# Running log-sum-exp over a sequence: the new last row is summed in place, one Ln takes all rows of a chunk, and GpSimd copies a part of that row to the work tile

## The chip, the cores and the metric

The kernel runs on one core of one Trainium2 chip. The metric is the device time in microseconds (us), the median of the runs shown. Engines are named as in the profile: PE is TensorE, DVE is VectorE, ACT is ScalarE, POOL is GpSimd, SP is SyncE, which here issues every transfer.

## The reference

The input x has 4 sequences of 4096 rows, each row with 4128 float32 numbers. The output is the running log-sum-exp along the rows.

```python
out[:, 0, :] = x[:, 0, :].copy()
for t in range(1, S):
    mx = np.maximum(out[:, t - 1, :], x[:, t, :])
    out[:, t, :] = mx + np.log(np.exp(out[:, t - 1, :] - mx) + np.exp(x[:, t, :] - mx))
```

## The kernel before

The kernel computes Ln of a running sum of Exp(x). At the end it tests from sums collected on the way (`probe`, `short`) whether the range of float32 was kept, and runs a slow general form if it was not.

The work is cut into 49 steps. A step takes r = 2 or 3 consecutive rows for each of the 128 partitions, all 4128 columns: partition p holds rows p·r to p·r + r − 1 of the block. A 2-row tile has 4128 KB (4.227 MB), a 3-row tile 6192 KB (6.340 MB). The lists `begin`, `usual` and `final` give r for each step: the first sequence begins 2, 2, 2, 3, 2, 3, and the last one ends 3, 3, 2, 2. Four tiles (`slots`) are used in turn; each is loaded, worked on in place and stored from.

Within a step there are three chunks of 1376 columns. In the texts chunks are numbered through: step 0 has chunks 0 to 2, step 1 has 3 to 5. A chunk goes through five operations:

- `exp` (line 102, ACT): Exp of all r rows in place. In the first step of a sequence line 105 adds a small check.
- `sums` (DVE): for three rows line 114 adds row 0 to row 1 in place. Then line 116 writes the sum of all the partition's rows to partitions 0 to 126 of the work tile `z`. Partition 127 of `z` keeps the last total of the step before.
- `head` (line 124, PE): a matrix product with a triangular matrix gives in PSUM, for each partition, the sum of all that comes before it, with the carried total from partition 127.
- `add` (DVE): line 133 adds that base from PSUM to rows 0 to r − 2. Line 141 adds rows r − 2 and r − 1 and writes the new last row to `z` (line 136, with the sum for `probe`, in the last step of a sequence).
- `log` (ACT): line 146 takes Ln of rows 0 to r − 2 in place, line 147 takes Ln of `z` and writes it to row r − 1.

The order on each engine is written out by hand in lists and fixed under a manual schedule. For most steps `usual_turn` gives this order. On ACT: Ln of chunk i, Exp of chunk i + 3, Ln of chunk i + 1, Exp of chunk i + 4, and so on. On DVE: add of chunk i, sums of chunk i + 2, add of chunk i + 1, sums of chunk i + 3. `last_turns` changes this for the last steps. SP's queue carries, in order, store t (line 91, after the three `log` of step t) and then load t + 3 (line 88, after store t − 1, which frees its tile). Steps 0 to 3 are loaded at the start; store 1 is issued ahead of load 4.

`needs` is a table from which the program order is derived; the waits themselves follow from what each instruction reads and writes. GpSimd sets constants and zeroes `z` at the start (lines 44 to 69) and has nothing after that.

Of the kernel before, what the change touches and what calls it, by code (L numbers as in the profile page):

```python
# [9 lines left out]
ACT = mybir.ActivationFunctionType  # L10
ALU = mybir.AluOpType
AX = mybir.AxisListType
P = 128
MM = 512
NC = 3
SLOTS = 4
SMALL = 2.0 ** -63
LARGE = 2.0 ** 62
# [3 lines left out]
def kernel(  # L22
# [5 lines left out]
    nc = tc.nc  # L28
    B, S, D = x.shape
    assert S % P == 0 and D % (NC * 32) == 0  # L30
    CH = D // NC
    cuts = [(s, min(s + MM, CH)) for s in range(0, CH, MM)]
# [13 lines left out]
        out=below, in_=below, pattern=[[1, P]], compare_op=ALU.is_ge,  # L46
# [5 lines left out]
        out=carried, in_=below, pattern=[[0, P]], compare_op=ALU.not_equal,  # L52
# [4 lines left out]

    probe = consts.tile([P, B * NC], FP32, name="probe")
    nc.gpsimd.memset(probe, 1.0)

    short = consts.tile([1, B * NC], FP32, name="short")
    spare = consts.tile([1, CH + 8], FP32, name="spare")[:, :CH]
# [3 lines left out]

    z = [zpool.tile([P, CH], FP32, name=f"z{c}") for c in range(NC)]
    for t in z:
        nc.gpsimd.memset(t, 0.0)  # L69

    slots = [x2.tile([P, 2, D], FP32, name="x0")]
    slots += [x3.tile([P, 3, D], FP32, name=f"x{k}") for k in range(1, SLOTS)]
    sides = [ppool.tile([P, CH], FP32, name=f"p{k}") for k in range(2)]
# [19 lines left out]
    class Chunk:  # L93
        def __init__(self, step, c):
            self.t, self.c, self.z = step, c, z[c]
            self.pt = sides[(step.n * NC + c) % 2]
            self.cols = slice(c * CH, (c + 1) * CH)
# [30 lines left out]
        def add(self):  # L128
            t, r = self.t, self.t.r
            k = t.b * NC + self.c  # L130
            e = t.xt[:, 0:r - 1, self.cols]
            base = self.pt.unsqueeze(1).to_broadcast([P, r - 1, CH])
            nc.vector.tensor_tensor(out=e, in0=base, in1=e, op=ALU.add)  # L133
            ends = (t.xt[:, r - 2, self.cols], t.xt[:, r - 1, self.cols])
            if t.last:
                nc.vector.tensor_tensor_reduce(  # L136
                    out=self.z, in0=ends[0], in1=ends[1], scale=1.0, scalar=0.0,
                    op0=ALU.add, op1=ALU.add, accum_out=probe[:, k:k + 1],
                )
            else:  # L140
                nc.vector.tensor_tensor(out=self.z, in0=ends[0], in1=ends[1], op=ALU.add)  # L141

        def log(self):
            t, r = self.t, self.t.r
            e = t.xt[:, 0:r - 1, self.cols]
            nc.scalar.activation(e, e, ACT.Ln)  # L146
            nc.scalar.activation(t.xt[:, r - 1, self.cols], self.z, ACT.Ln)  # L147

    begin = [2, 2, 2, 3, 2, 3, 2, 3, 2, 3, 3, 3, 2]
    usual = [3, 2, 3, 2, 3, 3, 3, 2, 3, 3, 3, 2]  # L150
# [2 lines left out]
    for b in range(B):  # L153
        row = 0
        for r in final if b == B - 1 else usual if b else begin:
            if row == S:
                break
            steps.append(Step(b, row, r, slots[len(steps) % SLOTS], row + P * r == S))
            steps[-1].n = len(steps) - 1
# [5 lines left out]

    moves = [("load", t) for t in range(SLOTS)]
    ahead = SLOTS
    for t in range(n):
# [25 lines left out]
    for t in range(n):  # L194
        exps, sums = last_turns.get(t, usual_turn)
# [11 lines left out]
    def needs(what, t, c=None):  # L207
        if what == "load":
            return [("store", t - SLOTS)]
        if what == "store":  # L210
            return [("log", t, c) for c in range(NC)]
        return {
            "exp": [("load", t)],
            "sums": [("exp", t, c), ("log", t - 1, c)],
            "head": [("sums", t, c), ("add", t - 1, c)],
            "add": [("head", t, c)],
            "log": [("add", t, c)],
        }[what]

    done, at = set(), {e: 0 for e in lists}  # L220
    while any(at[e] < len(l) for e, l in lists.items()):
        before = len(done), sum(at.values())
        for e, l in lists.items():
            while at[e] < len(l):
                op = l[at[e]]
                if op[1] < n:
                    if any(0 <= d[1] and d not in done for d in needs(*op)):
                        break
                    done.add(op)
                    of = steps[op[1]]  # L230
                    getattr(of if len(op) == 2 else of.chunks[op[2]], op[0])()
                at[e] += 1
        assert before != (len(done), sum(at.values()))
# [5 lines left out]
        out=fits[:, :B * NC], in0=probe, scalar1=LARGE, scalar2=None, op0=ALU.is_le,  # L239
    )  # L240
    nc.vector.tensor_scalar(
        out=fits[0:1, B * NC:], in0=short, scalar1=0.0, scalar2=None, op0=ALU.is_le,
# [7 lines left out]
        out=flag, in0=good, scalar1=float(P), scalar2=None, op0=ALU.is_lt,  # L250
# [62 lines left out]
```

## Time and profile before

| | |
|---|---|
| device time, median of 3 runs | 1260.83 us (1260.6 to 1261.09) |
| span of the profiled execution (first to last instruction) | 1258.4 us |
| what lies around the span, against the median | 2.4 us |
| ACT busy | 955.4 us |
| DVE busy | 956.2 us |
| PE busy | 602.4 us |
| POOL busy | 4.6 us |
| bytes moved by DMA, mean rate | 541.28 MB, 430 GB/s |
| ACT L146 and L147, Ln, mean of one | 2045 ns and 1334 ns |
| DVE L141, new last row, mean of one | 1592 ns |
| store 0, store 1, store 2, store 48 issued at | 38.04, 52.73, 70.28, 1239.89 us |

The profile is of one execution. Times in it are counted from the start of its span; the time of a whole execution is the span and what lies around it. Its groups mix shapes where a line has two: L146 takes 1376 elements a partition in a 2-row step and 2752 in a 3-row step. A transfer is shown where it is issued; its landing is later.

### The profile page before, as it was taken

To read this page: it belongs to the slowest core of one execution; us is meant where nothing else is said; L and a number is where in the kernel's file an instruction comes from. 1 tells how busy PE (TensorE), PEld (TensorE's weight loads), DVE (VectorE), ACT (ScalarE), POOL (GpSimd) and SP (SyncE) were. 2 spreads that over 40 slices of the span, in tenths; PEclk is the share of its full clock that TensorE was granted. 3 is DMA by queue.
4 is the path that set the end of the run, shared out by engine and by line. 5 is a ranking of instruction groups with operands and counts; after the bars stand their busy time and mean duration, and the time that the engine had idled before them with its cause. 6 is when DMAs were issued, how large, how long until landed. Compare 5 with 4: busy or idle time off the path is not lost.

```text
span 1258.4 us, 3228 instructions
## 1 busy us (share of the span) xinstructions
PE 602.4 (48%) x884; PEld 233.1 (19%) x884; DVE 956.2 (76%) x548; ACT 955.4 (76%) x466; POOL 4.6 (0%) x14
## 2 busy tenths in 40 slices
PE   3654454453535455345364535634535553463361
PEld 1221121121212122112121212211211211121120
DVE  3997696795967699579596679957957976795792
ACT  6987687786976699578697668866968966896792
POOL 1000000000000000000000000000000000000000
PEclk9877776676677667666676666766766776676676
DMA  9999999999999999999999999999999999999998
GB/s 403 420 439 426 432 436 428 432 437 429 439 425 438 430 437 433 436 435 427 440 422 436 436 432 434 434 430 435 437 428 437 431 435 431 434 437 433 432 435 354
DMA packets 14131, 541.28 MB, mean 430 GB/s; under 512 B 1568, under 2 KB 1568, under 8 KB 1568
## 3 DMA queue, kind: packets, MB, share of 16 engines
q1 hardware_dynamic: 14112, 541.07, 99.6%
q8 instruction: 7, 0.11, 0.0%
q14 instruction: 12, 0.10, 0.0%
HBM read 270.53 MB, written 270.53 MB: 430 GB/s over the span
## 4 chain that ended last, share of the span: by engine, by line
DMA 69%; ACT 14%; DVE 13%; PE 1%; issue 1%; SPq 0%; ACTq 0%; DVEq 0%
DMA x<-in_x_dram 52%; DMA out_dram<-x 17%; ACT x L102 6%; DVE x L133 5%; ACT x L146 5%; DVE z L116 3%; ACT x L147 3%; DVE z L141 3%; DVE x L114 2%; PE p L124 1%; SPq L91 0%; DVE z L136 0%; ACTq L146 0%; ACTq L254 0%; SPq L88 0%
## 5 line engine op out<-in xcount | busy, mean ns | idle before, releaser
L124 PE MATMUL p<-z,carried 128*128 128x512 f32 (+1 forms) x810 | 551.8, 842 | 544.3 <-DVE z L116 544.3
L102 ACT ACTIVATE x<-x 128x4128 f32<-128x4128 f32 (+1 forms) x147 | 468.0, 3187 | 219.7 <-DMA x<-in_x_dram 219.7
L124 PEld LDWEIGHTS p<-z,carried 128*128 128x128 f32 x810 | 213.4, 280 | 882.2 <-DVE z L116 648.3
L133 DVE TENSOR_TENSOR x<-p,x 128x2752 f32<-128x2752 f32 (+1 forms) x147 | 361.9, 2462 | 6.2 <-PE p L124 6.2
L146 ACT ACTIVATE x<-x 128x2752 f32<-128x2752 f32 (+1 forms) x147 | 300.6, 2045 | 63.5 <-DVE z L141 58.5
L114 DVE TENSOR_TENSOR x<-x 128x1376 f32<-128x1376 f32 x90 | 142.9, 1588 | 216.5 <-ACT x L102 216.5
L116 DVE TENSOR_TENSOR z<-x 127x1376 f32<-127x1376 f32 x147 | 233.9, 1591 | 53.8 <-ACT x L102 49.4
L141 DVE TENSOR_TENSOR z<-x 128x1376 f32<-128x1376 f32 x135 | 215.0, 1592 | 4.6
L147 ACT ACTIVATE x<-z 128x1376 f32<-128x1376 f32 x147 | 196.0, 1334 | 0.0
L124 PE MATMUL p<-z,below 128*128 128x512 f32 (+1 forms) x72 | 50.4, 864 | 87.4 <-DVE z L116 87.4
L124 PEld LDWEIGHTS p<-z,below 128*128 128x128 f32 x72 | 19.6, 289 | 117.7 <-DVE z L116 78.8
L136 DVE CUSTOM_DVE_ANT_0 z<-x 128x1376 f32<-128x1376 f32 x12 | 19.1, 1592 | 0.4
L105 ACT ACTIVATE spare<-x,tiny 1x1376 f32<-1x1376 f32 x12 | 17.3, 1442 | 0.5
L69 POOL MEMSET z<- 128x1376 f32 x3 | 3.7, 1241 | 0.0
L105 ACT ACTIVATION_READ_ACCUMULATOR spare<-x,tiny 1x1 f32 x12 | 2.2, 186 | 0.0
L247 PE MATMUL good<-ones,low 128*1 128x1 f32 x2 | 0.2, 164 | 3.8 <-DVE low L245 3.8
L34 ACT ACT_TABLE_LOAD x1 | 1.3, 1283 | 0.8 <-PEq L297 0.8
L136 DVE DVE_READ_ACCUMULATOR2_ANT probe<- 128x1 f32 x12 | 1.0, 83 | 0.0
L247 PEld LDWEIGHTS good<-ones,low 128*1 128x1 f32 x2 | 0.1, 80 | 4.8 <-DVE low L245 4.8
L249 DVE TENSOR_SCALAR flag<-good 1x1 int32<-1x1 f32 x1 | 0.1, 148 | 0.3 <-PE good L247 0.3
L51 POOL TENSOR_SCALAR_AFFINE_SELECT carried<-below 128x128 f32<-128x128 f32 x1 | 0.3, 290 | 0.0
L45 POOL TENSOR_SCALAR_AFFINE_SELECT below<-below 128x128 f32<-128x128 f32 x1 | 0.3, 285 | 0.0
(13 smaller groups left out, 1.6 us busy)
## 6 DMA issues: line engine op xcount, KB each, us to landing
x<-in_x_dram SPq DMA_DIRECT2D x30, 6192.0 KB, 38.4
out_dram<-x SPq DMA_DIRECT2D x30, 6192.0 KB, 25.0
x<-in_x_dram SPq DMA_DIRECT2D x19, 4128.0 KB, 33.0
out_dram<-x SPq DMA_DIRECT2D x19, 4128.0 KB, 21.6
```

What stands on the lines that cost most here:

```text
L34: nc.scalar.preload_act_table_set("natural_log_exp_and_others")
L69: nc.gpsimd.memset(t, 0.0)
L102: nc.scalar.activation(e, e, ACT.Exp)
L105: nc.scalar.activation(spare, t.xt[0:1, 0, self.cols], ACT.Relu, bias=tiny, scale=-1.0, accum_out=short[:, k:k + 1],)
L114: nc.vector.tensor_tensor(out=e[1], in0=e[0], in1=e[1], op=ALU.add)
L116: nc.vector.tensor_tensor(out=self.z[0:n], in0=e[r - 2][0:n], in1=e[r - 1][0:n], op=ALU.add,)
L124: nc.tensor.matmul(pt[:, a:b], lhsT=w, rhs=self.z[:, a:b], start=True, stop=True,)
L133: nc.vector.tensor_tensor(out=e, in0=base, in1=e, op=ALU.add)
L136: nc.vector.tensor_tensor_reduce(out=self.z, in0=ends[0], in1=ends[1], scale=1.0, scalar=0.0, op0=ALU.add, op1=ALU.add, accum_out=probe[:, ...
L141: nc.vector.tensor_tensor(out=self.z, in0=ends[0], in1=ends[1], op=ALU.add)
L146: nc.scalar.activation(e, e, ACT.Ln)
L147: nc.scalar.activation(t.xt[:, r - 1, self.cols], self.z, ACT.Ln)
```

## The change

The new last row is written in place, to row r − 1 of the tile, instead of to `z`. So one Ln takes all r rows of a chunk, and line 147 of before is gone. Since `head` of the next step still needs the last total in partition 127 of `z`, GpSimd copies partitions 96 to 127 of the new row to `z`, in every step but the last of a sequence (135 copies). `sums` of the next step then writes over partitions 0 to 126. Ln overwrites the row that the copy reads, so Ln waits for the copy; `sums` writes where the copy wrote, so it waits for the copy too. The order of the remaining instructions on PE, DVE, ACT and SP is the one of before. In the changed file the lines from 16 on stand one lower, those of `add` after the branch differ: line 142 is the new last row, line 143 the copy, line 147 the Ln.

```diff
+TOP = 96
...
             if t.last:
                 nc.vector.tensor_tensor_reduce(
-                    out=self.z, in0=ends[0], in1=ends[1], scale=1.0, scalar=0.0,
+                    out=ends[1], in0=ends[0], in1=ends[1], scale=1.0, scalar=0.0,
                     op0=ALU.add, op1=ALU.add, accum_out=probe[:, k:k + 1],
                 )
             else:
-                nc.vector.tensor_tensor(out=self.z, in0=ends[0], in1=ends[1], op=ALU.add)
+                nc.vector.tensor_tensor(out=ends[1], in0=ends[0], in1=ends[1], op=ALU.add)
+                nc.gpsimd.tensor_copy(out=self.z[TOP:], in_=ends[1][TOP:])

         def log(self):
-            t, r = self.t, self.t.r
-            e = t.xt[:, 0:r - 1, self.cols]
+            e = self.t.xt[:, :, self.cols]
             nc.scalar.activation(e, e, ACT.Ln)
-            nc.scalar.activation(t.xt[:, r - 1, self.cols], self.z, ACT.Ln)
...
-            "sums": [("exp", t, c), ("log", t - 1, c)],
+            "sums": [("exp", t, c), ("add", t - 1, c)],
```

## The prediction

> **What bounds the kernel now.** I read the page's engine shares first, then its slices and DMA rows, then the waits, then the stretches that lead up to the first and the last stores, and last the timeline of VectorE, ScalarE and SyncE.
>
> The head of the page and its DMA part:
>
> ```profile
> PE 602.4 (48%) x884; PEld 233.1 (19%) x884; DVE 956.2 (76%) x548; ACT 955.4 (76%) x466; POOL 4.6 (0%) x14
> ...
> DMA  9999999999999999999999999999999999999998
> ...
> q1 hardware_dynamic: 14112, 541.07, 99.6%
> ```
>
> VectorE and ScalarE are each idle for a quarter of the span; the one queue's transfers fill it. So 541.07 MB over the DMA engines is the bound (433 GB/s over 100 to 1170 us), and only a stretch in which the queue runs dry adds time. Work saved on ScalarE or VectorE cannot shorten it.
>
> The waits say the same from the other end (columns: who waited, for whom, us in total, times, longest):
>
> ```profile
> ACT x L102 <- DMA x<-in_x_dram: 219.7, 43, 11.9
> ...
> ACT x L146 <- DVE z L141: 58.5, 65, 5.0
> ```
>
> What must be known is how near the queue comes to running dry. At each store I take the bytes issued so far (a 2-row tile is 4.227 MB, a 3-row tile 6.340) less the bytes moved, from stretches that begin at 0 and end at the issue (columns: length, busy time of PE, PEld, DVE, ACT, POOL, clock, DMA share, GB/s):
>
> ```profile
> 0.00:52.73 52.73, 24.31 (x44) 10.07 (x45) 32.17 (x21) 40.29 (x28) 4.64 (x14) 0.94 0.98 410
> 0.00:70.28 70.28, 35.04 (x60) 13.97 (x60) 48.02 (x31) 57.38 (x37) 4.64 (x14) 0.88 0.98 414
> 0.00:92.87 92.87, 47.16 (x81) 18.93 (x82) 70.25 (x43) 76.83 (x46) 4.64 (x14) 0.86 0.99 421
> ...
> 0.00:1239.89 1239.89, 602.36 (x884) 233.11 (x884) 956.23 (x548) 955.36 (x466) 4.64 (x14) 0.69 1.00 432
> ```
>
> Store 1 at 52.73: issued 23.25 MB (four loads, store 0), moved 0.410 x 52.73 = 21.62, left 1.63 MB, at 430 GB/s 3.8 us. So the queue would run dry at 56.5. In the same way store 2 has 6.1 us in hand, store 3 7.4, and the last store, at 1239.89, about 2.8. In mid-run the stores come with 5 to 13 us in hand. The margins are thin in two places: the first three stores, whose steps run as fast as ScalarE and VectorE let them, and the end.
>
> The timeline of ScalarE in the first stretch (start, us, engine, line, shape):
>
> ```profile
> 30.48 1.33 ACT L146 ACTIVATE x<-x 128x1376 f32<-128x1376 f32 x1
> 31.72 1.33 ACT L147 ACTIVATE x<-z 128x1376 f32<-128x1376 f32 x1
> 32.96 2.48 ACT L102 ACTIVATE x<-x 128x2752 f32<-128x2752 f32 x1
> 35.42 1.35 ACT L146 ACTIVATE x<-x 128x1376 f32<-128x1376 f32 x1
> ```
>
> It shows no gap, and a chunk every 4.9 us. VectorE beside it:
>
> ```profile
> 33.74 1.59 DVE L141 TENSOR_TENSOR z<-x 128x1376 f32<-128x1376 f32 x1
> 35.48 1.59 DVE L116 TENSOR_TENSOR z<-x 127x1376 f32<-127x1376 f32 x1
> ```
>
> L141 ends at 35.33, and L146, which needs it, starts at 35.42. The next sums start at 35.48, as the Exp they need ends. Whatever is put between L141 and the Ln lies on the path.
>
> **The change, part by part.** *Last row in place (L141, L136).* Same operands in, another place out: 1592 ns stays, cost nothing, and nothing has to hide it.
>
> *One Ln in place of two.* 147 instructions fewer. The two start 2.50 us apart from the next Exp (30.48 to 32.96), where one instruction on 2752 elements has a pitch of 2.40 (48.7 us of ScalarE's idle time already falls ahead of L146, so little of the 147 x 0.10 = 15 us can show). It counts where ScalarE sets the pace: 0.1 us a chunk.
>
> *Sums wait for the copy, not for the Ln.* The page has no wait of L116 on L147, so that gains nothing. The copy of a chunk is issued a whole add ahead of the next sums on that z (4.8 us for two rows), so the new wait is covered unless the copy takes longer than that.
>
> *The GpSimd copy, 135 times.* GpSimd is otherwise empty after 5.3 us, so nothing queues behind a waiting copy but the next copy. The Ln now waits for it, since it overwrites the row that the copy reads; behind the Ln on ScalarE is queued the next step's Exp, behind that the sums, and behind the third chunk's Ln the store on SP's queue, with the next load after it. The trace has no copy. From below, a memset that only writes:
>
> ```profile
> L69 POOL MEMSET z<- 128x1376 f32 x3 | 3.7, 1241 | 0.0
> ...
> L51 POOL TENSOR_SCALAR_AFFINE_SELECT carried<-below 128x128 f32<-128x128 f32 x1 | 0.3, 290 | 0.0
> ```
>
> From above, the affine select, which reads and writes: less the 98 ns of the smallest memset it is 1.50 ns an element, so 0.10 + 1376 x 1.50 = 2.16 us. A copy does no comparing and is nearer to the memset: I take 1.4, and 0.1 for one more hand-off (L141 to L146 takes 0.09), 1.5 together. Both ends stay open, and no gain is possible, since the Ln waits for more than before. The Trainium skill ("GPSIMD Engine Reference", § 4.1 Engine selection) calls one-input operations there roughly line-rate; at its 1.2 GHz an estimate is 1.15 us, which would make each sum below some 0.5 us smaller; no run so far shows a copy.
>
> *What that does to the pace.* The orders close a ring over two chunks: Ln of chunk i, Exp of i+3, sums of i+3, both adds of i+2, Ln of i+2. Two rows, now: 2.50 + 2.56 + 1.50 + 1.62 + 1.68 = 9.9, and the trace has 35.42 - 25.60 = 9.8. With the copy: 9.8 - 0.1 + 1.5 = 11.2. Three rows: 15.2 becomes 16.6, while the queue takes 19.7 for two such chunks and 13.1 for two 2-row chunks. So the copy alone does not change the bound of mid-run.
>
> *Where the copy falls.* It is released at the end of L141. In this ring that is, for every other chunk, the moment at which the next sums start on VectorE, an add with two SBUF operands. The trace has no GpSimd read beside a VectorE add: its memsets are over at 5.3 us, the first add starts at 15.67. If the two take turns, the copy waits 1.6 us more (the add's 1.59; with three rows it gets in between L114 and L116), or holds the add up by its own 1.4. The ring is then 11.2 + 1.6 = 12.8 for two rows and 18.2 for three, still under 13.1 and 19.7. Sharing of any kind, a turn for either or both slowed, costs about this; only full independence costs none. I take the turns.
>
> **The sum, with turns.** First stretch: Ln of chunk 0 from 25.60 to 28.6 (sums until 27.06, copy), then every second 12.8 later: chunk 2 at 41.4, 4 at 54.2, 6 at 67.0. Chunks 1, 3, 5 follow 4.8 behind: 33.4, 46.2, 59.0. Store 1 comes at 59.0 + 2.5 = 61.5, 5.0 us after the queue runs dry at 56.5. Store 1 and load 4 are 8.45 MB or 19.7 us, to 81.2. The Exp behind the Ln of chunk 6 is the first with three rows and ends at 73.0; sums (3.2) and the adds of chunk 8 (3.2) end at 79.5, its copy waits out L114 and its Ln starts at 82.6, so store 2 goes out at 85.1: 3.9 dry. Store 2 and load 5 last 24.6 us, to 109.7; the Ln of chunk 11 starts at 107.1, store 3 at 110.8: 1.1 dry. Together 10.0.
>
> Mid-run: a store that follows a landing is delayed by 1.5 + 1.6 = 3.1 us, against at least 4.7 in hand. The store after it comes at the engines' pace, three chunks of 9.1 instead of 7.3 (271.69 to 293.50), so 5.5 + 3.1 = 8.6 late against 12 in hand. Nothing.
>
> End, from the last but two loads' landing at 1178.72: no copies in the last step, but the ring over the two steps ahead delays store 47 by 5.3 us against 4.9 in hand, and the last by 4.2 against 2.8: about 1.5.
>
> Sum: 11.5 on 1258.4, the span, is 1269.9. The profiled execution's span lies 2.4 below the median of 1260.83, which I keep: **1272**. Its own range is 1266 (the copy at 1.24 and short turns) to 1280 (2.16).
>
> **The rivals.** *No turns: not slower.* Copy and add run side by side. The ring is 11.2; Ln of chunk 5 starts at 54.5, store 1 at 57.0 (0.5 dry), store 2 at 77.6 against 76.7 (0.9), store 3 at 100.6 against 102.3, the end 1.1 late with 2.8 in hand. That is +1.4, 1262, within 0.2% (2.5 us, about what a measurement of this kernel can tell from no change). For it: VectorE's adds stay within 1583 to 1594 ns whatever ScalarE, PE and the queue do beside them. Against: none of these is GpSimd. It tips at a copy of 1.7 us; at 2.16 it is +4.5, 1265.
>
> *The turn covers both sums of a three-row step.* The 30 ns between L114 and L116 may be too short for GpSimd to get in. Then the three-row ring is 19.8, and 20.5 with the dear copy, against 19.7: mid-run is bound by the engines. Over 45 pairs of chunks that is 6 to 36 us more, and 3 in the first stretch: 1281 to 1311, about 1290.
>
> On turns as such, the Trainium skill ("SBUF — State Buffer", § Who interferes with whom) says that a Vector instruction with two SBUF inputs contends with a GpSimd instruction that reads SBUF, and that the second one blocks for the whole instruction. By that rule one of the two slower cases holds; no run here shows it yet.
>
> *Faster.* Needs the queue to move bytes faster, as nothing else bounds. The 10-us stretches swing between 404 and 466 GB/s with no pattern that later stores would change: to 1257, and little chance.
>
> **How the numbers follow.** Turns between single instructions 0.52; turns over both sums 0.10; independent with a cheap copy 0.26, with a dear one 0.08; faster 0.04. Slower by over 0.2% is 0.52 + 0.10 + 0.08 = 0.70, within 0.26, faster 0.04. The range runs from 1259.5, under the independent case, to 1286, which leaves out the upper half of the second rival: about 0.1 outside, and some for what I have not seen.
>
> **What would show it.** Right: copies of 1.2 to 2.2 us, many that start 1.6 after L142 ends or adds of 3 us; Ln waiting on GpSimd some 135 times; store 1 near 61 and store 2 near 85; a dip below 410 GB/s in slices 2 and 3 and the old rate from 4 on. Wrong: all copies starting at L142's end and adds at 1.59 (then 1262), or idle queue time between 130 and 1170 us (then 1285 and up).

## The result, and the profile after

The changed kernel takes 1280.44 us (median of 5 runs, 1279.17 to 1285.87) against 1261.09 us before (5 runs): ratio 1.0165, 95% interval 1.0152 to 1.0177. That is 19.4 us more, from the medians; 11.2 were forecast, and the result lies inside the range. The changed kernel also scatters more: its five runs lie within 6.7 us, those of the kernel before within 0.7. The profiled execution took 1279.17 us with a span of 1277.4, against 1258.4.

The head of the page of the changed kernel:

```profile
PE 620.0 (49%) x884; PEld 242.4 (19%) x884; DVE 1008.4 (79%) x548; ACT 941.1 (74%) x319; POOL 272.9 (21%) x149
...
GB/s 405 373 372 416 420 429 435 433 434 424 435 427 435 433 443 420 428 435 430 417 425 435 439 427 435 432 421 438 436 410 433 429 430 429 435 432 420 435 400 365
...
q1 hardware_dynamic: 14112, 541.07, 99.0%
```

Before, the slices and the two sums on VectorE stood like this:

```profile
GB/s 403 420 439 426 432 436 428 432 437 429 439 425 438 430 437 433 436 435 427 440 422 436 436 432 434 434 430 435 437 428 437 431 435 431 434 437 433 432 435 354
...
L114 DVE TENSOR_TENSOR x<-x 128x1376 f32<-128x1376 f32 x90 | 142.9, 1588 | 216.5 <-ACT x L102 216.5
L116 DVE TENSOR_TENSOR z<-x 127x1376 f32<-127x1376 f32 x147 | 233.9, 1591 | 53.8 <-ACT x L102 49.4
```

The bytes are the same, ScalarE is 14 us less busy, and VectorE is 52 us busier with the same 548 instructions. The rate is down to 373 and 372 GB/s in the second and third slices (420 and 439 before), and a little lower on the whole in the rest.

Its groups (line, engine, operation, count; busy us, mean ns; idle before, releaser):

```profile
L147 ACT ACTIVATE x<-x 128x4128 f32<-128x4128 f32 (+1 forms) x147 | 469.4, 3194 | 230.6 <-POOL z L143 228.1
...
L143 POOL COPY z<-x 32x1376 f32<-32x1376 f32 x135 | 268.2, 1987 | 978.2 <-DVE x L142 756.3
...
L117 DVE TENSOR_TENSOR z<-x 127x1376 f32<-127x1376 f32 x147 | 281.8, 1917 | 97.1 <-ACT x L103 86.7
L115 DVE TENSOR_TENSOR x<-x 128x1376 f32<-128x1376 f32 x90 | 145.0, 1611 | 146.8 <-ACT x L103 145.8
```

ScalarE now waits 228 us for the copy ahead of its Ln (before, 58.5 us for VectorE). The sums at L117 (L116 before) have grown from 1591 ns to 1917, those at L115 (L114) from 1588 to 1611. Why shows in the timeline of the first stretch, VectorE and GpSimd (start, us; in brackets how long the engine was idle, and for what):

```profile
37.57 1.59 DVE L117 TENSOR_TENSOR z<-x 127x1376 f32<-127x1376 f32 x1
37.66 2.70 POOL L143 COPY z<-x 32x1376 f32<-32x1376 f32 x1 [6.46 <-DVE x L142]
...
40.70 1.59 DVE L142 TENSOR_TENSOR x<-x 128x1376 f32<-128x1376 f32 x1
42.53 1.33 POOL L143 COPY z<-x 32x1376 f32<-32x1376 f32 x1 [2.18 <-DVE x L142]
```

and in a three-row step:

```profile
253.17 1.58 DVE L115 TENSOR_TENSOR x<-x 128x1376 f32<-128x1376 f32 x1
253.41 2.54 POOL L143 COPY z<-x 32x1376 f32<-32x1376 f32 x1 [11.81 <-DVE x L142]
254.86 2.53 DVE L117 TENSOR_TENSOR z<-x 127x1376 f32<-127x1376 f32 x1
```

All copies together (ns, shortest/median/longest):

```profile
L143 POOL COPY z<-x x135: 1332/2452/2786, 25.3 to 1249.2; 32x1376 f32<-32x1376 f32 x135
```

With VectorE idle a copy takes 1.33 us. Released together with an add that has two SBUF operands it takes 2.4 to 2.8: it is shown from its release, waits for the add and then runs. 65 copies take 1.33, 70 take 2.4 to 2.8, and none lies between. In the three-row step it gets in between L115 and L117, and L117 is then shown as 2.53. They take turns, one instruction each. That is what the Trainium skill says ("SBUF — State Buffer", § Who interferes with whom: contention with a GpSimd instruction that reads SBUF, the second one blocked). In these rows the second one also gets its turn between two adds that are shown 0.1 us apart (254.75 to 254.86).

The bytes moved up to stores 1, 2 and 3 of the changed kernel (last column GB/s):

```profile
0.00:60.25 60.25, 25.35 (x43) 10.45 (x44) 32.11 (x21) 39.77 (x22) 16.44 (x20) 0.84 0.92 386
0.00:83.27 83.27, 38.25 (x62) 15.56 (x63) 50.69 (x32) 56.60 (x28) 22.91 (x23) 0.81 0.91 381
0.00:108.16 108.16, 50.80 (x80) 20.34 (x81) 72.29 (x43) 75.73 (x34) 29.67 (x26) 0.79 0.94 391
```

Store 1 goes out at 60.25, when 0.386 x 60.25 = 23.26 MB have moved: all 23.25 that were issued. At stores 2 and 3 it is 31.7 of 31.7 and 42.3 of 42.3. The queue is empty at all three.

### The profile page after: what moved, and what is told of

It reads as the page before. It is cut to its first block, busy times and chain, and to the rows that moved or that the text cites. A ratio compares the mean times of both kernels' runs of the same rounds, so it can differ in the third digit from the quotient of the medians.

```text
span 1277.4 us, 3500 instructions
## 1 busy us (share of the span) xinstructions
PE 620.0 (49%) x884; PEld 242.4 (19%) x884; DVE 1008.4 (79%) x548; ACT 941.1 (74%) x319; POOL 272.9 (21%) x149
## 4 chain that ended last, share of the span: by engine, by line
DMA 35%; ACT 28%; DVE 23%; POOL 8%; issue 2%; PE 2%; SPq 0%; POOLq 0%; DVEq 0%; ACTq 0%
DMA x<-in_x_dram 35%; ACT x L147 14%; ACT x L103 13%; DVE x L134 8%; POOL z L143 8%; DVE z L117 6%; DVE x L142 5%; DVE x L115 4%; PE p L125 2%; ACT spare L106 1%; SPq L92 0%; DVE x L137 0%; POOLq L143 0%; DVEq L117 0%; SPq L89 0%
## 5 line engine op out<-in xcount | busy, mean ns | idle before, releaser
L125 PE MATMUL p<-z,carried 128*128 128x512 f32 (+1 forms) x810 | 568.8, 865 | 567.0 <-DVE z L117 567.0
L147 ACT ACTIVATE x<-x 128x4128 f32<-128x4128 f32 (+1 forms) x147 | 469.4, 3194 | 230.6 <-POOL z L143 228.1
L103 ACT ACTIVATE x<-x 128x4128 f32<-128x4128 f32 (+1 forms) x147 | 467.7, 3185 | 91.1 <-DMA x<-in_x_dram 91.1
L143 POOL COPY z<-x 32x1376 f32<-32x1376 f32 x135 | 268.2, 1987 | 978.2 <-DVE x L142 756.3
L125 PEld LDWEIGHTS p<-z,carried 128*128 128x128 f32 x810 | 222.2, 292 | 915.1 <-DVE z L117 670.8
L117 DVE TENSOR_TENSOR z<-x 127x1376 f32<-127x1376 f32 x147 | 281.8, 1917 | 97.1 <-ACT x L103 86.7
L115 DVE TENSOR_TENSOR x<-x 128x1376 f32<-128x1376 f32 x90 | 145.0, 1611 | 146.8 <-ACT x L103 145.8
L142 DVE TENSOR_TENSOR x<-x 128x1376 f32<-128x1376 f32 x135 | 215.0, 1592 | 4.7
L137 DVE CUSTOM_DVE_ANT_0 x<-x 128x1376 f32<-128x1376 f32 x12 | 19.1, 1592 | 0.4
```

Source lines behind the costliest of these rows:

```text
L103: nc.scalar.activation(e, e, ACT.Exp)
L115: nc.vector.tensor_tensor(out=e[1], in0=e[0], in1=e[1], op=ALU.add)
L117: nc.vector.tensor_tensor(out=self.z[0:n], in0=e[r - 2][0:n], in1=e[r - 1][0:n], op=ALU.add,)
L125: nc.tensor.matmul(pt[:, a:b], lhsT=w, rhs=self.z[:, a:b], start=True, stop=True,)
L137: nc.vector.tensor_tensor_reduce(out=ends[1], in0=ends[0], in1=ends[1], scale=1.0, scalar=0.0, op0=ALU.add, op1=ALU.add, accum_out=probe[: ...
L142: nc.vector.tensor_tensor(out=ends[1], in0=ends[0], in1=ends[1], op=ALU.add)
```

## The experiments

The medians, each against the kernel before in the same session:

| kernel | us | more than before, us | ratio, 95% interval |
|---|---|---|---|
| changed | 1280.44 | 19.4 | 1.0152 to 1.0177 |
| steps 0 to 5 alone | 1270.29 | 9.6 | 1.0063 to 1.0091 |
| steps 6 to 43 alone | 1269.40 | 8.7 | 1.0057 to 1.0084 |
| steps 44 to 48 alone | 1261.12 | 0.4 | 0.9993 to 1.0011 |
| memset in place of the copy | 1263.84 | 3.0 | 1.0015 to 1.0035 |
| changed, with two Ln | 1268.08 | 7.3 | 1.0037 to 1.0065 |
| before, with an idle copy | 1261.66 | 0.8 | 1.0000 to 1.0017 |
| before, stores delayed by 3.2 us | 1273.26 | 12.6 | 1.0085 to 1.0116 |
| the same by 2.5 us | 1269.42 | 8.6 | 1.0032 to 1.0075 |
| the same by 1.3 us | 1260.66 | -0.2 | 0.9991 to 1.0009 |
| changed, loads ahead of stores | 1439.58 | 178.8 | 1.1396 to 1.1427 |
| before, loads ahead of stores | 1415.97 | 155.1 | 1.1211 to 1.1243 |
| 3.2 us, loads ahead of stores | 1415.51 | 154.7 | 1.1217 to 1.1248 |

**Where it is lost: three parts alone.** The same change, in a range of steps:

```diff
+FROM, TO = 0, 6          # 6, 44 and 44, 99 in the two others
...
+            new = FROM <= t.n < TO
...
+                    out=ends[1] if new else self.z, in0=ends[0], in1=ends[1], op=ALU.add,
+                )
+                if new:
+                    nc.gpsimd.tensor_copy(out=self.z[TOP:], in_=ends[1][TOP:])
...
```

Outside the range each step has the two Ln and the wait of the kernel before.

> The change in steps 0 to 5 alone, the old form in steps 6 to 48. Theory (turns between the copy and VectorE's two-operand adds, felt where the queue runs dry): the first stretch holds +10 us, so 1271 (1269 to 1273), with the queue dry before stores 1 and 2, and from 150 us on the curve of bytes moved stays 10 us behind that of before. Rival (the loss is one of pace over the whole run, and a late start would be made up by the idle quarter of the engines): below 1266.

> The change in steps 6 to 43 alone. The prediction had nothing here; the trace of the whole change loses 7 us between 60 and 515 MB moved. Theory (stores that go out with under 3 us in hand cost some time although the sum of bytes in hand is not zero): +6 to +8, so 1267 to 1269, some 2.2 us for each sequence of 12 steps. Rival (mid-run loses only because the run starts late and the margins never recover): within 2 us of before, 1261 to 1263.

> The change in steps 44 to 48 alone. Theory: the end's own share of the 19 us, +1.5 to +3, so 1262.5 to 1264; the last store is issued 4 to 7 us later than before, of which the bytes in hand hide most. Rival (the end loses as much as the 5 us by which the late stores 46 to 48 found the queue empty): 1266.

9.6, 8.7 and 0.4 us: 18.7 of the 19.4, so the parts add up within the noise. The first part is the size that was expected. Mid-run is a little above the 6 to 8 expected. The end was expected at 1.5 to 3 and costs nothing that a run can tell. With the end alone changed, the last store goes out at 1244.21 instead of 1239.89, and the span is 0.9 us longer: what was in hand covers it.

**What the turns cost: the same wait without a read.** The copy becomes a memset of as many elements that the Ln waits for in the same way.

```diff
-                nc.gpsimd.tensor_copy(out=self.z[TOP:], in_=ends[1][TOP:])
+                nc.gpsimd.memset(ends[1][TOP:], 1.0)
```

> The whole change, but GpSimd's copy is a memset of the same 32 x 1376 elements of the new last row: as long, at the same place, and the Ln waits for it in the same way, but it reads nothing (left out: the carry to the next step, and a quarter of the last rows' values; the sums do not wait for GpSimd any more). Theory (the copy's read and the adds with two SBUF operands take turns): no add over 1.6 us, every memset 1.24, the ring at 11.2 for two rows, so 1261 to 1265. Rival (what costs is only that the Ln waits for one more engine, whatever that does): 1277 to 1282, as the whole change.

1263.84. The timeline shows the memset beside the sums, with neither held up:

```profile
36.81 1.59 DVE L117 TENSOR_TENSOR z<-x 127x1376 f32<-127x1376 f32 x1
36.87 1.24 POOL L143 MEMSET x<- 32x1376 f32 x1 [5.25 <-ACT x L103]
```

So a Ln that waits for 1.24 us of GpSimd costs 3.0 us, and the other 16.4 need the read. The 3.0 are lost at the first stores: store 1 goes out at 56.83, when the queue is empty (0.409 x 56.83 = 23.24 MB moved of 23.25), and from 150 us on the rate is that of before (433 GB/s, shown below). Two differences besides the read are left. The 0.09 us between 1.24 and 1.33 are too little to matter. The sums no longer wait for GpSimd, but in the changed kernel's list of waits no wait of the sums (L117) for the copy shows either. The Trainium skill ("SBUF — State Buffer", § Who interferes with whom) excepts an instruction that only writes, and this trace agrees: all 135 memsets take 1.24 us, and no sum at L117 takes over 1.6.

**Who pays for the turns: the copy without a waiting Ln.** This is the kernel before with a copy of the same size to a tile that nobody reads.

```diff
-    spare = consts.tile([1, CH + 8], FP32, name="spare")[:, :CH]
+    scrap = consts.tile([P, CH + 8], FP32, name="spare")
+    spare = scrap[0:1, :CH]
...
                 nc.vector.tensor_tensor(out=self.z, in0=ends[0], in1=ends[1], op=ALU.add)
+                nc.gpsimd.tensor_copy(out=scrap[96:, :CH], in_=self.z[96:])
```

> The kernel before, with two Ln and the new last row in z, and a copy by GpSimd of the same 32 x 1376 elements after each line that makes the new last row, from z to an unused tile, 135 times; no Ln waits for it, only the next sums on that z. Theory (the copy is dear because Exp and store stand behind a Ln that waits for it): copies of 1.3 to 2.8 us and held-up adds as in the changed kernel, but 1261 to 1264. Rival (VectorE's time lost in the turns is the price): 1270 or more.

1261.66, 0.8 more. The page of this kernel has the copies and the held-up sums at full price:

```profile
L117 DVE TENSOR_TENSOR z<-x 127x1376 f32<-127x1376 f32 x147 | 320.3, 2179 | 38.4 <-ACT x L103 29.2
...
L143 POOL COPY spare<-z 32x1376 f32<-32x1376 f32 x135 | 283.7, 2101 | 938.3 <-DVE z L142 938.3
```

VectorE loses 86 us at L117 (233.9 before) and the time hardly moves. Turns alone are nearly free; a Ln that waits alone costs 3 us; together they cost 19.

**Two Ln again, the first of which does not wait for the copy.**

```diff
-            e = self.t.xt[:, :, self.cols]
+            t, r = self.t, self.t.r
+            e = t.xt[:, 0:r - 1, self.cols]
             nc.scalar.activation(e, e, ACT.Ln)
+            l = t.xt[:, r - 1, self.cols]
+            nc.scalar.activation(l, l, ACT.Ln)
```

> The whole change with the Ln cut in two again: rows 0 to r-2 first, which waits for VectorE alone, then the last row in place, which waits for the copy. Theory (the copy is dear because the one Ln stands behind it): the first Ln covers 1.3 (two rows) or 2.5 us (three) of a copy of 1.3 to 2.7, the ring is some 11.2 for two rows and unchanged for three; copies and adds still take turns; 1262 to 1267. Rival (the turns cost VectorE's time, whoever waits): 1277 or more, since the adds are held up as often.

1268.08, so 12 us of the 19 come back; that is 1.1 us above the expected 1262 to 1267. In the two-row steps the first Ln is shorter than a held-up copy, and the second still waits:

```profile
43.18 1.35 ACT L148 ACTIVATE x<-x 128x1376 f32<-128x1376 f32 x1 [0.89 <-DVE x L142]
43.33 2.46 POOL L143 COPY z<-x 32x1376 f32<-32x1376 f32 x1 [4.81 <-DVE x L142]
...
45.82 1.35 ACT L150 ACTIVATE x<-x 128x1376 f32<-128x1376 f32 x1 [1.29 <-POOL z L143]
```

**What mid-run loses: late stores are enough.** The kernel before, its stores delayed by memsets on a row that nobody reads again but the store (these kernels give up the values of that row):

```diff
             nc.scalar.activation(t.xt[:, r - 1, self.cols], self.z, ACT.Ln)
+            if self.c == NC - 1 and 6 <= t.n < 44:
+                for w in (CH, CH, CH // 2):     # (CH, CH) and (CH,) in the two others
+                    nc.gpsimd.memset(t.xt[:, r - 1, D - w:], 1.0)
```

> The kernel before; in steps 6 to 43 GpSimd overwrites the last row of the third chunk with a constant after its Ln (three write-only memsets, 1.24 + 1.24 + 0.6 us), so that the store and the load behind it go out 3.2 us later, and no other engine changes its work. Theory (a late store costs time by itself when it leaves under 3 us in hand): +5 to +8, 1266 to 1269, as in the mid-run part alone. Rival (the prediction's rule: 4.7 us in hand cover a delay of 3.1, and mid-run's loss comes from the engines' pace or from GpSimd's reads): 1261 to 1262.

> The kernel of the delayed stores with one memset in place of three (a delay of 1.3 in place of 3.2 us; the overwritten row is the same). Theory (a threshold: in the runs so far a store with 4 us in hand lost nothing, one with 1.5 to 2.5 lost 0.5 to 0.8): 3.4 us or more stay in hand, so 1261 to 1264. Rival (each microsecond of delay costs in proportion): 12.6 x 1.3 / 3.2 = 5, so 1266.

> The kernel of the delayed stores with two memsets (2.5 us) in place of three (3.2) or one (1.3); the overwritten row is the same. With one nothing was lost, with three 12.6 us. Theory (a floor of some 3 us in hand under which a store costs time): about 2 us stay in hand at the thinnest stores, so a part of the loss, +3 to +8, 1264 to 1269. Rival (the loss has to do with the third memset itself): 1260 to 1262.

A delay of 3.2 us costs 12.6, more than the 5 to 8 expected and more than the whole mid-run part of the change, though ScalarE and VectorE do what they did. One of 1.3 costs nothing, and in proportion it would have been 5. One of 2.5 costs 8.6, just above the 3 to 8 expected, and lies on the edge: its eight runs are spread from 1260.82 to 1272.91, where those of the kernel before lie within 1.3 us. The rate from 150 to 1170 us is the last column of the stretches that follow, one kernel each. Before:

```profile
150.00:1170.00 1020.00, 489.96 (x699) 188.67 (x700) 784.79 (x440) 778.37 (x369) 0.00 (x0) 0.67 1.00 433
```

The delay of 1.3 us:

```profile
150.00:1170.00 1020.00, 494.49 (x699) 189.99 (x700) 784.12 (x440) 778.28 (x369) 47.29 (x38) 0.67 1.00 433
```

The delay of 3.2 us:

```profile
150.00:1170.00 1020.00, 478.27 (x686) 184.02 (x687) 771.94 (x434) 771.75 (x367) 120.18 (x114) 0.67 1.00 428
```

Steps 6 to 43 alone:

```profile
150.00:1170.00 1020.00, 492.38 (x688) 192.07 (x689) 819.54 (x435) 762.95 (x254) 205.37 (x103) 0.67 1.00 430
```

The memset in place of the copy:

```profile
150.00:1170.00 1020.00, 501.05 (x702) 193.17 (x700) 783.25 (x440) 765.30 (x251) 132.71 (x107) 0.67 1.00 433
```

1 GB/s less over these 1020 us is 2.4 us. The DMA share stays at 1.00 in all of them: no gap shows, the same engines that count as busy move less. Store 10 may stand for the thin ones, those with the least in hand. Issued before it are 118.36 MB; less the bytes moved up to its issue there are in hand

| kernel | store 10 at | GB/s from 0 | in hand, us | rate 150 to 1170 | long packets, us |
|---|---|---|---|---|---|
| before | 271.69 | 427 | 5.5 | 433 | 0.8 |
| memset in place of the copy | 275.47 | 423 | 4.3 | 433 | 0.8 |
| delay 1.3 | 272.48 | 428 | 4.0 | 433 | 0.9 |
| changed, with two Ln | 278.05 | 421 | 3.0 | 432 | 5.0 |
| delay 2.5 (its slowest run) | 274.73 | 427 | 2.4 | 428 | 11.8 |
| changed | 285.12 | 412 | 2.1 | 430 | 7.9 |
| delay 3.2 | 274.98 | 428 | 1.6 | 428 | 12.9 |
| steps 6 to 43 alone | 275.23 | 428 | 1.3 | 430 | 9.0 |

(in hand good to 0.4 us, by the rounding of the rate). With 4 us at store 10 nothing is lost, with 3 or less something is. At other stores the kernel with the 1.3 us delay comes closer: by the same working from its packets, store 17 goes out with 3.0 us in hand and store 21 with 3.1, and still nothing is lost. So the edge is near 3 us, and one store does not decide the time: the delay of 2.5 loses more than the changed kernel, which has less in hand at store 10. The delayed kernel has more thin stores: 12 and 24 go out with 2.2 and 2.3 us in hand, where the changed kernel has 5.7 and 5.9.

The last column is read from the packets of the transfers in each trace, and it shows where the time went. Between 150 and 1170 us a packet of a three-row transfer takes 1829 ns (median) in every one of these kernels, one of a two-row transfer 1222. Before, 39 of 9945 packets take over 100 ns more than that; with the delay of 3.2 us 369 do, and the longest takes 3267 ns. The column is what these long packets take beyond the median, spread over the 16 engines. Less the 0.8 of before, it comes close to what mid-run lost in each kernel. So most packets are as fast as before and a few are slower; the busy share does not show it, because a long packet counts as busy.

**Filling the queue earlier: a miss.** Load t + 3 goes ahead of store t.

```diff
     for t in range(n):
+        first = 1 <= t < 44 and ahead < n      # 6 <= t < 44 in the two others
+        if first:
+            moves.append(("load", ahead))
+            ahead += 1
         moves.append(("store", t))
-        if t and ahead < n:
+        if t and ahead < n and not first:
...
```

> The whole change, and on SP's queue load t+3 goes ahead of store t in steps 1 to 43 (it needs only store t-1). ScalarE, VectorE and GpSimd keep their work and order, so copies and adds still take turns. Theory (the loss is that the queue is thinly filled when a store goes out): with the load already queued at each store the mid-run part of 8 us goes, and of the first stretch's 10 some 3 to 5 (load 4 no longer waits behind store 1): 1264 to 1270. Rival (the engines' ring, longer by the turns, sets the pace of mid-run): 1276 or more.

> The kernel before, with load t+3 ahead of store t in steps 6 to 43. Theory: with 4.7 us and more in hand before, nothing is lost there, so nothing is to be won: 1260 to 1262. Rival (even before, mid-run loses some time at thin stores): 1255 to 1259, a version faster than both.

> The kernel of the delayed stores (before, with memsets on the last row of the third chunk in steps 6 to 43, which delay store t by 3.2 us), with load t+3 ahead of store t in those steps. Theory (the 12.6 us came from the thin queue at the store): 1260.5 to 1263. Rival (the memsets or the later landing of the store cost by themselves): 1270 or more.

All three expectations were wrong, by 140 us and more; that two of the rivals were open upwards is no hit, since their reason is not the one that shows. I had taken the load for one that is ready when its turn comes. SP's waits in the kernel before, with loads ahead:

```profile
SPq L88 <- DMA out_dram<-x: 1176.2, 42, 33.6
SPq L91 <- ACT x L147: 146.8, 18, 24.3
```

Load t + 3 needs store t − 1 landed, and SP's queue is in order: the finished store t now stands behind that landing, and the transfers run dry there in nearly every step: the DMA share from 150 to 1170 us falls from 1.00 to 0.92. In the order as it was, SP waited 973 us for the Ln and 73 us for landings. Since all three are bound by this, they tell nothing of the delays or the turns. That late stores are also what the changed kernel loses in mid-run rests on the delayed stores and the table above: the size fits, but no run took the late stores away and kept the turns. No run of this case is faster than the kernel before.

## Why the prediction was right, point by point

**The turns.** The likeliest case was the one that held. Copy 1.4 was 1.33 (the estimate of 1.15 was low); the wait for one add is there, in about every other copy as told (70 of 135), but inside the copy's own time and not as a later start. The ring over two chunks was put at 12.8 us and is 12.6 (Ln starts at 27.81, 40.39, 52.95, 65.53); the three-row ring at 18.2 is 17.9 (255.99, 273.96, 291.84). The chunks between found VectorE idle, as the sum had it.

**The first stretch, 10.0.** Store 1 was put at 61.5 and came at 60.25, store 2 at 85.1 and came at 83.27, store 3 at 110.8 and came at 108.16, each with the queue dry. Changed alone, these steps cost 9.6.

**Mid-run, 0: the term that was mis-sized.** It measured 8.7 alone. The delays themselves were about as told (in hand at store 10 are 2.1 us instead of 5.5, 3.4 less, where 3.1 was told), and the three-row ring stayed under the queue's 19.7 us, so the second rival, the turn over both sums, did not come. What failed is the rule behind the term, that a delay is free as long as the sum of bytes in hand outlasts it. The delayed stores show that the last 3 us or so in hand are not free. 4.7 less 3.1 leaves 1.6, which is under that. With it a sign that the prediction named for being right did not come: the old rate did not return from slice 4 on (430 GB/s from 150 to 1170 us, 433 before).

**The end, 1.5.** Alone it measured 0.4, within its interval of no change. The store times were near (the last one 4.3 us late alone, 4.2 told); the 2.8 in hand understate what covers it. From the issue of the last store to the end of the span it took 18.5 us before (1239.89 to 1258.4) and 13.3 in the changed kernel (1264.07 to 1277.4), where the queue was empty. These two leave some 5 us of transfers ahead of it, where the mean over the 16 engines gave 2.8.

**The sum.** 10.0 + 0 + 1.5 against 9.6 + 8.7 + 0.4. Right in mechanism and in the first place, 8 us short in the second. The measured time lies just above the likeliest case's own range, which ended at 1280, and inside the whole one only because that reached up to 1286 for the second rival, which did not come. That part is luck. One reading was off as well: the idle time ahead of L146 that VectorE ends is 58.5 us in the row shown, not 48.7; no term of the sum rests on it.

**The rivals.** Without turns the forecast was +1.4; the memset, which has no turns, measured +3.0. So a wait without turns is small, as this rival had it, though twice its size. Its store times were near: store 1 told at 57.0 and seen at 56.83, store 2 at 77.6 and 76.5.

**What is not settled.** Why a store with 1 to 3 us in hand makes some packets long while no gap shows in the DMA share. One explanation is that the bytes in hand are a mean over 16 engines: in the trace of before the sixteen completion events of one transfer lie 4.6 us apart (median), so some engines run out well ahead of the mean. That would fit an edge of this size, but no run here took the spread away, and the place of the long packets does not speak for it. With steps 6 to 43 alone they lie some 12 to 18 and 27 to 35 us behind the thin stores 10, 18, 22 and 34, about where the store and the load that is issued with it end, and not at the thin store itself. So that late stores cost time is shown, and the way in which they do is open.

## What to carry to other kernels

Before work is moved to an idle engine, look at what its instruction reads and what the neighbour does at the moment of its release: a GpSimd copy beside VectorE's two-operand adds takes its turn, and it matters as soon as something in order waits for it. In a kernel that is bound by its transfers, work out for each issue how many microseconds of transfers are still in hand; a delay is free only down to an edge, here near 3 us, not to zero. And an issue queue in order is as late as the least ready of its heads: moving a transfer forward in it needs the time at which it is ready, not the time at which one would like it.

## What the runs showed of the hardware that was not expected

A blocked instruction is shown as a longer one: copies of 1.33 us as 2.4 to 2.8, adds of 1.59 as up to 2.60 (up to 2.77 with two Ln), so busy time rose by 52 us on VectorE with no work added. A memset at the same place lengthens neither. The same holds for transfers: what late stores cost shows as a few packets of up to 3.4 us in place of 1.83, at an unchanged busy share. And near the edge one kernel varies from run to run: with stores 2.5 us late it took between 1260.82 and 1272.91 us, as fast as without a delay at one end and as slow as with the full one at the other.
